# A decoder trunk on one core: the last steps of each layer norm taken through a PSUM bank, with nothing of them on GpSimd

## The chip, the cores and the metric

The kernel runs on one core of one Trainium2 chip. The metric is the device time of one execution in microseconds. A core has five engines, each with a queue of its own that it works through in order: TensorE (PE), which multiplies matrices and writes only to PSUM; VectorE (DVE); ScalarE (ACT); GpSimd (POOL); and SyncE (SP), which here only issues DMAs. Semaphores order the engines against each other. SBUF is the working memory; PSUM consists of eight banks per partition.

## The reference, cut to what matters

The reference is a stack of two decoder layers over 528 tokens (16 meta tokens and 512 tokens of the sequence), 1024 wide. Each layer has a half-step SwiGLU feed-forward block, a token mixer with three kinds of heads, and a second feed-forward block; behind each of the three stands a layer norm.

```python
def _layer_norm(x, g, b):
    xf = x.astype(F32)
    mu = jnp.mean(xf, axis=-1, keepdims=True)
    var = jnp.mean(jnp.square(xf - mu), axis=-1, keepdims=True)
    return ((xf - mu) * lax.rsqrt(var + LN_EPS) * g.astype(F32) + b.astype(F32)).astype(x.dtype)
...
    for l in range(DEPTH):
        h = _layer_norm(DEEPNORM_ALPHA * h + FFN_RES * _swiglu(h, ffn_w_gate[l, 0], ffn_w_up[l, 0], ffn_w_down[l, 0]),
                        ln_g[l, 0], ln_b[l, 0])
...
        mix = jnp.concatenate([o_lru, o_ssd, o_dn], axis=-1) @ w_out[l]
        h = _layer_norm(DEEPNORM_ALPHA * h + mix, ln_g[l, 1], ln_b[l, 1])
        h = _layer_norm(DEEPNORM_ALPHA * h + FFN_RES * _swiglu(h, ffn_w_gate[l, 1], ffn_w_up[l, 1], ffn_w_down[l, 1]),
                        ln_g[l, 2], ln_b[l, 2])
    return h[:, N_META:]
```

## The kernel before, in words

The tokens are cut into two halves, u = 0 (272 tokens) and u = 1 (256 tokens). Activations lie transposed: 128 channels on the partitions, eight tiles `m` for the 1024 channels, tokens along the row. A product in fp32 accuracy is made of three products of shortened numbers: each operand is split into a high part and a low part, `hh` and `hl` for the activations, and two halves of a `wt` tile for the weights. One product of a 128-column weight slab with the activations (`gemm`) is 24 matmuls into one tile `g` of PSUM: first the eight with the high weights and `hh`, then eight with the low weights and `hh`, and last eight with the high weights and `hl`. A slab comes by DMA into `wr`; ACT makes its high part, and POOL (four pieces) or DVE (one piece) the low part.

PSUM is dealt out in two pools: three banks with the tag `g` for these products, and five banks with the tag `c` for everything else: sums of the norms, and the small products of the mixer (the SSD blocks `ssd_block`, with tiles `s`, `s_sm`, `s_st`; the DeltaNet chain with `d_` and `db` tiles; the LRU).

A layer norm (`layer_norm`) of a half works on its eight tiles `acc[u][:, m]`: a matmul with ones gives the sum on all partitions (`mu`, a `c` bank); the tiles are centred, squared and summed (`ls`, `lq`); a chain of some fifteen tiny DVE steps on the tile `lv` makes the inverse root; matmuls of `lv` with the identity spread it over the partitions (`rp`, a `c` bank; in the trace `c<-ident,lv`). Then, for each of eight tiles: DVE scales it in place (`acc<-acc,par,c`), ACT adds the bias into `hh` (`hh<-acc,par`), DVE forms the low part `hl` as tile plus bias minus `hh` (`hl<-acc,par,hh`), and ACT adds the bias into the tile itself for the next residual (`acc<-acc,par`). For the tile m = 5 (`LN_POOL`) the last two are the other way about: ACT writes the tile, and POOL subtracts (`hl<-acc,hh`). There are ten such norms: three places in each of two layers, for two halves, less the last place, which another function does.

The order of the instructions on every engine is made at build time by a planner (`Recorder.schedule`). All instructions are recorded, each with a price from a table and a level, the length of what hangs on it; then the planner runs a clock for each engine and issues, where an engine is free, the ready instruction with the highest level. Tiles take a buffer of their pool when their first instruction is issued. A `c` tile that is not the oldest one still without a bank gets one only if more than three of the five are free (`SPARE`). Where the planner sees TensorE idle before a new `g` tile, it may put in matmuls of ones with ones (line 388), which compute nothing that is used. The two halves run a stage apart and are woven together, so that the products of one half fill TensorE while the mixer or the norm of the other goes through its chain.

Of the kernel before, what the change touches and what calls it, by code (L numbers as in the profile page):

```python
# [8 lines left out]
F32 = mybir.dt.float32  # L9
F32R = mybir.dt.float32r  # L10
I32 = mybir.dt.int32
AF = mybir.ActivationFunctionType
ALU = mybir.AluOpType
AX = mybir.AxisListType

P = 128
D = 1024
KD = 8
# [14 lines left out]
TILES = 6  # L33
DB_BUFS = 2
LRU_BUFS = 1
LN_POOL = (5,)
GROUPS = ((3, 3, 3, 3, 2), (3, 3, 3, 3, 2))
ALONE = ((2, 2, 2, 2), (2, 2, 2, 2))
POOL_SHARE = 0.7
# [360 lines left out]
class Trunk:  # L400
# [391 lines left out]
    def layer_norm(self, u, s, row, off=0, keep=False):  # L792

        nc = self.nc
        n = NTOK[u] - off
        a = [self.acc[u][:, m, off:] for m in range(KD)]
        mu = self.tl(self.psm, [P, 512], "c")[:, :n]
        nc.tensor.matmul(mu, self.ones, s, start=True, stop=True)
        s2 = [self.tl(self.wk, [P, 272], "ls2")[:, :n] for _ in range(2)]
        for m in range(KD):  # L800
            nc.vector.scalar_tensor_tensor(a[m], mu, -1.0 / D, a[m], ALU.mult, ALU.add)
            if m < 2:
                nc.scalar.activation(s2[m], a[m], AF.Square)
            else:
                q = self.tl(self.wk, [P, 272], "lq")[:, :n]
                nc.scalar.activation(q, a[m], AF.Square)
                if m % 2:
                    nc.gpsimd.tensor_tensor(s2[1], s2[1], q, ALU.add)
                else:
                    nc.vector.tensor_tensor(s2[0], s2[0], q, ALU.add)  # L810
        blocks = []
        c = 0
        while c < n:
            w = (n % P) if (c == 0 and n % P) else P
            blocks.append((c, w))
            c += w
        nb = len(blocks)
        vp = self.tl(self.psm, [P, 512], "c")
        v = self.tl(self.wk, [P, 3, 3], "lv")
        nc.vector.memset(v, 1.0)  # L820
        for i, (c, w) in enumerate(blocks):
            for q in range(2):
                nc.tensor.matmul(vp[:w, i:i + 1], s2[q][:, c:c + w], self.ones[:, 0:1], start=q == 0, stop=q == 1)
        if blocks[0][1] < P:
            w = blocks[0][1]
            nc.vector.tensor_scalar(v[:w, 0, 0:1], vp[:w, 0:1], 1.0 / D, LN_EPS, ALU.mult, ALU.add)
            nc.vector.tensor_scalar(v[:, 0, 1:nb], vp[:, 1:nb], 1.0 / D, LN_EPS, ALU.mult, ALU.add)
        else:
            nc.vector.tensor_scalar(v[:, 0, :nb], vp[:, :nb], 1.0 / D, LN_EPS, ALU.mult, ALU.add)
        self.rsqrt(v[:, 1, :], v[:, 0, :], v[:, 2, :])  # L830
        rp = self.tl(self.psm, [P, 512], "c")[:, :n]
        for i, (c, w) in enumerate(blocks):
            nc.tensor.matmul(rp[:, c:c + w], v[:w, 1, i:i + 1].to_broadcast([w, P]), self.ident[:w, :w], start=True, stop=True)
        g = [self.col(ROW_LN_G + row + m) for m in range(KD)]
        b = [self.col(ROW_LN_B + row + m) for m in range(KD)]
        hi = [self.hh[u][:, m, off:] for m in range(KD)]
        for m in range(KD):
            nc.vector.scalar_tensor_tensor(a[m], a[m], g[m], rp, ALU.mult, ALU.mult)
            nc.scalar.activation(hi[m], a[m], AF.Identity, bias=b[m])
        for m in range(KD):  # L840
            lo = self.hl[u][:, m, off:]
            if m in LN_POOL:
                nc.scalar.activation(a[m], a[m], AF.Identity, bias=b[m])
                nc.gpsimd.tensor_tensor(lo, a[m], hi[m].bitcast(F32), ALU.subtract)
            else:
                nc.vector.scalar_tensor_tensor(lo, a[m], b[m], hi[m].bitcast(F32), ALU.add, ALU.subtract)
                nc.scalar.activation(a[m], a[m], AF.Identity, bias=b[m])
        if keep:
            nc.sync.dma_start(self.res[u], self.acc[u])

# [790 lines left out]
```

## Time and profile before

| what | value |
|---|---|
| time, median of 3 runs | 2460.74 us (2446.69 to 2464.13) |
| the profiled execution: its time, its span | 2460.38 us, 2458.7 us |
| TensorE busy | 2312.6 us, 94% of the span |
| VectorE busy | 1504.2 us, 61% |
| ScalarE busy | 865.9 us, 35% |
| GpSimd busy | 883.0 us, 36% |
| mean granted clock of TensorE | 0.948 of full speed |

The span runs from the first to the last instruction; the time of the execution has 1.7 us more around it. The profile names an instruction by its line, its engine, and what it writes and reads (`hl<-acc,par,hh`). Since every instruction is issued by the planner, nearly all have line 390; the names of the tiles tell them apart. "Idle before" is the time that the engine stood still just ahead of an instruction, and the name behind the arrow is what it waited for. Matmuls overlap, so a row's duration is longer than what it adds: sixteen in 2.16 us begin 0.125 us apart.

### The profile page before, as it was taken

Reading aid. Unit: us, or ns where it says so; the run is one execution under the profiler, and the core shown is the slowest. Engines: PE = TensorE matmul, PEld = TensorE weight load, DVE = VectorE, ACT = ScalarE, POOL = GpSimd, SP = SyncE. Lnnn points to the kernel's source line nnn. Section 1 sums busy time; section 2 is a strip of 40 time slices with the busy share of each in tenths; the row PEclk is TensorE's granted clock in tenths of the full one; section 3 lists DMA queues with packets and bytes.
Section 4 is the critical chain, followed back from the end, with each engine's and each line's share of the span. In section 5 each row is a group of like instructions: output and inputs, shape, how many; then the busy total and the mean of one; then the engine's idle time right before and its main releaser. Section 6 shows DMA issues by size and latency. Waiting matters only on the chain.

```text
span 2458.7 us, 46832 instructions
## 1 busy us (share of the span) xinstructions
PE 2312.6 (94%) x18712; PEld 2199.1 (89%) x18712; DVE 1504.2 (61%) x3529; ACT 865.9 (35%) x1546; POOL 883.0 (36%) x1214
## 2 busy tenths in 40 slices
PE   8999998988899999999999999998989989999997
PEld 8999998876887999999999999988768878999996
DVE  6444467757867664444574444678577686654445
ACT  3222344442333454222242223443433444432222
POOL 5000566634545576000010005666445556640000
PEclk9999999987886999999999999999888989999999
DMA  6232454531341456233232334545314525552320
GB/s 169 78 103 87 131 145 144 146 97 35 110 108 54 139 157 186 86 104 95 68 95 80 91 91 138 156 139 141 97 35 118 142 61 155 172 168 90 91 90 35
DMA packets 426332, 271.99 MB, mean 111 GB/s; under 512 B 33421, under 2 KB 407921, under 8 KB 425857
## 3 DMA queue, kind: packets, MB, share of 16 engines
q1 hardware_dynamic: 425536, 268.83, 37.7%
q8 instruction: 147, 2.41, 0.4%
q0 software_dynamic: 576, 0.16, 0.1%
q14 instruction: 73, 0.59, 0.1%
HBM read 260.76 MB, written 8.19 MB: 109 GB/s over the span
## 4 chain that ended last, share of the span: by engine, by line
PE 70%; DVE 16%; DMA 4%; issue 3%; POOL 3%; ACT 3%; SPq 0%; POOLq 0%; DVEq 0%; ACTq 0%
PE g L390 61%; PE c L390 9%; POOL wt L390 2%; DVE wt L390 2%; DVE acc L390 2%; DVE fs L390 1%; DVE lru L390 1%; ACT wt L390 1%; DMA wr<-in_ffn_w_gate_dram 1%; DVE d_sq L390 1%; DVE s L390 1%; DMA wr<-in_ffn_w_up_dram 1%; DMA d_tx<-d_xd 1%; DVE sp L390 1%; DVE l_h L390 1%
## 5 line engine op out<-in xcount | busy, mean ns | idle before, releaser
L390 PE MATMUL g<-hh,wt 128*128 128x256 f32 (+1 forms) x7616 | 1063.7, 290 | 22.5 <-DVE fs L390 8.8
L390 PEld LDWEIGHTS g<-hh,wt 128*128 128x128 f32 x7616 | 985.4, 192 | 37.5 <-DVE fs L390 9.0
L390 POOL TENSOR_TENSOR wt<-wr,wt 128x256 fp32r<-128x256 f32 x884 | 681.8, 803 | 783.7 <-ACT wt L390 726.4
L390 ACT CAST wt<-wr 128x1024 fp32r<-128x1024 f32 x484 | 498.0, 1040 | 619.0 <-PE g L390 482.0
L390 PE MATMUL g<-hl,wt 128*128 128x256 f32 (+1 forms) x3808 | 562.7, 288 | 1.8 <-DVE hl L390 1.2
L390 PE MATMUL g<-hid,wt 128*128 128x256 f32 (+1 forms) x4224 | 543.7, 286 | 18.6 <-DVE hid L390 10.2
L390 PEld LDWEIGHTS g<-hid,wt 128*128 128x128 f32 x4224 | 524.4, 189 | 27.2 <-DVE hid L390 13.0
L390 PEld LDWEIGHTS g<-hl,wt 128*128 128x128 f32 x3808 | 505.3, 192 | 6.3 <-DVE hl L390 2.5
L390 DVE SCALAR_TENSOR_TENSOR acc<-g,acc 128x256 f32<-128x256 f32 (+1 forms) x608 | 256.7, 427 | 226.1 <-PE g L390 222.0
L390 DVE TENSOR_TENSOR wt<-wr,wt 128x1024 fp32r<-128x1024 f32 x263 | 335.0, 1285 | 88.1 <-ACT wt L390 86.8
L390 DVE SCALAR_TENSOR_TENSOR fs<-ft,g 128x272 f32<-128x272 f32 (+1 forms) x200 | 84.6, 423 | 188.8 <-ACT ft L390 188.0
L390 DVE TENSOR_TENSOR g<-fs,g 128x256 f32<-128x256 f32 (+1 forms) x176 | 76.4, 434 | 173.9 <-PE g L390 173.5
L390 ACT ACTIVATE ft<-g 128x272 f32<-128x272 f32 (+1 forms) x208 | 80.6, 388 | 281.6 <-PE g L390 249.2
L390 ACT CAST hid<-g 128x256 fp32r<-128x256 f32 (+1 forms) x176 | 65.8, 374 | 223.5 <-DVE g L390 223.2
L390 POOL TENSOR_TENSOR ls<-ls,lq 128x256 f32<-128x256 f32 (+1 forms) x30 | 27.6, 920 | 264.2 <-ACT lq L390 261.3
L390 DVE TENSOR_TENSOR hid<-g,hid 128x256 fp32r<-128x256 f32 (+1 forms) x176 | 74.9, 425 | 42.4 <-ACT hid L390 42.1
L390 POOL TENSOR_TENSOR wr<-wr,db 128x512 f32<-128x512 f32 x4 | 5.0, 1274 | 262.0 <-ACT wr L390 262.0
L390 DVE SCALAR_TENSOR_TENSOR fs<-g,par,fs 128x271 f32<-128x271 f32 (+1 forms) x144 | 69.1, 482 | 21.9 <-ACT halo L390 17.0
L390 ACT ACTIVATE fs<-g,par 128x272 f32<-128x272 f32 (+1 forms) x48 | 25.2, 524 | 67.4 <-PE g L390 57.9
L390 DVE SCALAR_TENSOR_TENSOR acc<-acc,par,c 128x256 f32<-128x256 f32 (+1 forms) x104 | 43.6, 480 | 8.6 <-PE c L390 8.5
L390 ACT ACTIVATE ft<-fs 128x272 f32<-128x272 f32 (+1 forms) x56 | 23.7, 423 | 58.6 <-DVE fs L390 58.6
L390 POOL TENSOR_TENSOR s<-s,s_sm 128x512 f32<-128x512 f32 (+1 forms) x20 | 22.0, 1105 | 61.6 <-ACT s L390 45.1
(305 smaller groups left out, 1742.4 us busy)
## 6 DMA issues: line engine op xcount, KB each, us to landing
wr<-in_ffn_w_gate_dram SPq DMA_DIRECT2D x120, 512.0 KB
wr<-in_ffn_w_up_dram SPq DMA_DIRECT2D x120, 512.0 KB
wr<-in_ffn_w_down_dram SPq DMA_DIRECT2D x120, 512.0 KB
wr<-in_w_in_dram SPq DMA_DIRECT2D x88, 512.0 KB
wr<-in_w_out_dram SPq DMA_DIRECT2D x32, 512.0 KB
res<-acc SPq DMA_DIRECT2D x2, 1088.0 KB
acc<-res SPq DMA_DIRECT2D x8, 272.0 KB
acc<-in_x_dram SPq DMA_DIRECT2D x4, 512.0 KB
```

Of the source, the lines that this page charges most:

```text
L390: op.fn(*[on(x) for x in op.args], **{k: on(x) for k, x in op.kw.items()})
```

## The change

The scaled tile is no longer written back in place, but into a `c` bank of PSUM of its own, one for each of the eight tiles. From that bank ACT takes `hh`, DVE takes `hl`, and ACT takes the sum that goes into the tile `acc`. All eight low parts are on DVE; the case for POOL is gone. The lines are written tile by tile, and the planner makes its order anew from the recorded instructions.

```diff
-LN_POOL = (5,)
...
         for m in range(KD):
-            nc.vector.scalar_tensor_tensor(a[m], a[m], g[m], rp, ALU.mult, ALU.mult)
-            nc.scalar.activation(hi[m], a[m], AF.Identity, bias=b[m])
-        for m in range(KD):
-            lo = self.hl[u][:, m, off:]
-            if m in LN_POOL:
-                nc.scalar.activation(a[m], a[m], AF.Identity, bias=b[m])
-                nc.gpsimd.tensor_tensor(lo, a[m], hi[m].bitcast(F32), ALU.subtract)
-            else:
-                nc.vector.scalar_tensor_tensor(lo, a[m], b[m], hi[m].bitcast(F32), ALU.add, ALU.subtract)
-                nc.scalar.activation(a[m], a[m], AF.Identity, bias=b[m])
+            t = self.tl(self.psm, [P, 512], "c")[:, :n]
+            nc.vector.scalar_tensor_tensor(t, a[m], g[m], rp, ALU.mult, ALU.mult)
+            nc.scalar.activation(hi[m], t, AF.Identity, bias=b[m])
+            nc.vector.scalar_tensor_tensor(self.hl[u][:, m, off:], t, b[m], hi[m].bitcast(F32), ALU.add, ALU.subtract)
+            nc.scalar.activation(a[m], t, AF.Identity, bias=b[m])
```

In the order, names carry numbers of their buffers: `acc_24_119` is the tile of half 0 and `acc_32_127` that of half 1; `c_121` to `c_125` are the five banks; one row of the matmuls stands for a run of alike ones (x8).

The first place is VectorE at the first norm of half 1 in layer 0 (538 us in the trace before). Before, from its scaling steps on:

```order
L390 SCALAR_TENSOR_TENSOR acc_32_127<-acc_32_127,par_103,c_123 128x256 x8
L390 TENSOR_TENSOR s_799_894<-c_121,t_y_630 16x512
L390 TENSOR_TENSOR s_800_895<-c_121,st_dtd_642 16x512
L390 TENSOR_TENSOR s_sm_899<-c_122,tri_105 16x16
L390 TENSOR_TENSOR s_sm_899<-c_123,tri_105 16x16
L390 SCALAR_TENSOR_TENSOR hl_5_100<-acc_32_127,par_103,hh_3_98 128x256 x7
L390 TENSOR_SCALAR s_806_901<-c_121,st_cs_641 16x16 x4
```

In the changed kernel, the end of the same norm (five scalings and four low parts stand ahead of these rows):

```order
L389 SCALAR_TENSOR_TENSOR c_121<-acc_32_127,par_103,c_123 128x256
L389 SCALAR_TENSOR_TENSOR hl_5_100<-c_125,par_103,hh_3_98 128x256
L389 SCALAR_TENSOR_TENSOR c_125<-acc_32_127,par_103,c_123 128x256
L389 SCALAR_TENSOR_TENSOR hl_5_100<-c_121,par_103,hh_3_98 128x256
L389 SCALAR_TENSOR_TENSOR c_121<-acc_32_127,par_103,c_123 128x256
L389 SCALAR_TENSOR_TENSOR hl_5_100<-c_125,par_103,hh_3_98 128x256
L389 TENSOR_TENSOR s_815_910<-c_123,t_y_638 16x512
L389 TENSOR_TENSOR s_816_911<-c_123,st_dtd_650 16x512
L389 TENSOR_TENSOR s_sm_915<-c_125,tri_105 16x16
L389 SCALAR_TENSOR_TENSOR hl_5_100<-c_121,par_103,hh_3_98 128x256
L389 TENSOR_TENSOR s_sm_915<-c_125,tri_105 16x16
L389 TENSOR_SCALAR s_822_917<-c_125,st_cs_649 16x16 x4
```

The first steps of half 0's SSD block (`s<-c,t_y` and the next ones) stood between the scalings and the low parts; now they stand behind all scalings and seven low parts, and the norm goes round on two banks, `c_121` and `c_125`, with `rp` in `c_123`. At the same norm of layer 1 (1763 us) the order changes in the same way, with all eight low parts ahead.

The second place is TensorE at the same norm. Before, from the last matmul of ones with `ls` to the first products of the SSD block:

```order
L390 MATMUL c_122<-ones_104,ls_480_575 128x1
L390 MATMUL g_145<-hh_2_97,wt_144 128x272 x7
L390 MATMUL g_145<-hl_4_99,wt_144 128x272 x8
L388 MATMUL c_123<-ones_104 128x128 x2
L390 MATMUL c_123<-ident_96,lv_876 128x128 x2
L390 MATMUL c_121<-ident_96,acc_24_119 16x128 x4
L390 MATMUL c_122<-ident_96,acc_24_119 16x128
L390 MATMUL c_122<-acc_24_119 16x16
L390 MATMUL c_123<-acc_24_119 16x16
L390 MATMUL c_121<-tri_105,st_adt_635 128x16 x2
```

In the changed kernel:

```order
L389 MATMUL c_121<-ones_104,ls_480_575 128x1
L389 MATMUL g_136<-hl_4_99,wt_135 128x272 x4
L389 MATMUL g_139<-hh_2_97,wt_158 128x272 x7
L389 MATMUL c_123<-ident_96,lv_884 128x128 x2
L389 MATMUL g_139<-hh_2_97,wt_158 128x272 x9
L389 MATMUL g_139<-hl_4_99,wt_158 128x272 x8
L389 MATMUL g_145<-hh_2_97,wt_133 128x272 x16
L389 MATMUL g_145<-hl_4_99,wt_133 128x272 x2
L389 MATMUL c_123<-ident_96,acc_24_119 16x128 x4
L389 MATMUL c_125<-ident_96,acc_24_119 16x128
L389 MATMUL c_125<-acc_24_119 16x16
L389 MATMUL g_145<-hl_4_99,wt_133 128x272 x6
```

The norm has moved ahead of products of half 0: 35 of their matmuls now stand between the spreading of `lv` and the SSD block's first products, where there was none, and six more behind those. Over the whole program the matmuls of ones on a `c` bank (line 388 before) go from 46 to 31, and those on a `g` bank from 13 to 12; every other matmul is there as often as before.

## Rows read from the trace of the kernel before

**Rows 1.** The page's head and part 1: busy time, share, instructions.

```profile
span 2458.7 us, 46832 instructions
PE 2312.6 (94%) x18712; PEld 2199.1 (89%) x18712; DVE 1504.2 (61%) x3529; ACT 865.9 (35%) x1546; POOL 883.0 (36%) x1214
```

**Rows 2.** The page's part 4: shares of the chain that ended last.

```profile
PE 70%; DVE 16%; DMA 4%; issue 3%; POOL 3%; ACT 3%; SPq 0%; POOLq 0%; DVEq 0%; ACTq 0%
```

**Rows 3.** The view of the cores: span and mean granted clock.

```profile
core 0: 2458.7 us, clock 0.948
```

**Rows 4.** Windows view: stretch, its length, each engine's busy time, PEclk.

```profile
538.90:576.50 37.60, 32.21 (x124) 21.20 (x125) 21.96 (x63) 12.52 (x30) 5.71 (x8) 0.50 0.14 43
```

**Rows 5.** Tile view of hl: min/median/max ns; then what its readers waited for.

```profile
L390 DVE SCALAR_TENSOR_TENSOR hl<-acc,par,hh x70: 464/492/1018, 365.6 to 2105.0; 128x256 fp32r<-128x256 f32 x42, 128x272 fp32r<-128x272 f32 x28
...
L390 POOL TENSOR_TENSOR hl<-acc,hh x10: 733/1068/3488, 365.8 to 2102.2; 128x256 fp32r<-128x256 f32 x6, 128x272 fp32r<-128x272 f32 x4
...
  DVE hl L390: 3.7, 8
...
  POOL hl L390: 1.4, 2
```

**Rows 6.** Groups of VectorE, all forms together: count, busy us, mean ns.

```profile
L390 DVE SCALAR_TENSOR_TENSOR acc<-acc,par,c 128x256 f32<-128x256 f32 (+1 forms) x104 | 43.6, 480 | 8.6 <-PE c L390 8.5
...
L390 DVE SCALAR_TENSOR_TENSOR hl<-acc,par,hh 128x256 fp32r<-128x256 f32 (+1 forms) x70 | 37.8, 597 | 0.0
```

**Rows 7.** Groups of ScalarE by form: count, busy us, mean ns.

```profile
L390 ACT ACTIVATE acc<-acc,par 128x256 f32<-128x256 f32 x48 | 21.2, 498 | 1.1 <-DVE hl L390 1.1
L390 ACT ACTIVATE hh<-acc,par 128x256 fp32r<-128x256 f32 x48 | 20.3, 496 | 2.9 <-DVE acc L390 2.9
...
L390 ACT ACTIVATE lru<-c,par 128x256 f32<-128x256 f32 x4 | 1.9, 474 | 3.9 <-DVE l_h L390 2.2 <-PE c L390 1.6
```

**Rows 8.** Timeline of TensorE at half 0's first norm: start, length, [idle before].

```profile
368.99 0.30 PE L390 MATMUL g<-hl,wt 128*16 128x272 f32 x1 [0.18 <-DVE hl L390]
369.88 0.42 PE L390 MATMUL g<-hl,wt 128*16 128x272 f32 x2 [0.59 <-DVE hl L390]
370.77 0.30 PE L390 MATMUL g<-hl,wt 128*16 128x272 f32 x1 [0.47 <-DVE hl L390]
```

**Rows 9.** Timeline of VectorE at half 1's first norm.

```profile
538.21 3.22 DVE L390 SCALAR_TENSOR_TENSOR acc<-acc,par,c 128x256 f32<-128x256 f32 x8
541.34 0.67 DVE L390 TENSOR_TENSOR s<-c,t_y 16x512 f32<-16x512 f32 x1
...
542.70 3.22 DVE L390 SCALAR_TENSOR_TENSOR hl<-acc,par,hh 128x256 fp32r<-128x256 f32 x7
545.85 1.21 DVE L390 TENSOR_SCALAR s<-c,st_cs 16x16 f32<-16x16 f32 x8
```

**Rows 10.** Timeline of TensorE at half 1's first norm.

```profile
527.30 2.16 PE L390 MATMUL g<-hh,wt 128*128 128x272 f32 x16
...
537.17 0.71 PE L390 MATMUL c<-ident,lv 128*128 128x128 f32 x4 [2.25 <-DVE lv L390]
...
541.48 0.23 PE L390 MATMUL c<-acc 64*16 64x16 f32 x2 [2.91 <-DVE acc L390]
542.67 3.59 PE L390 MATMUL c<-tri,st_adt 16*128 16x16 f32 x16 [0.95 <-DVE s L390]
```

**Rows 11.** The chain that ended last, in order of time: two of its pieces.

```profile
1263.81 2.29 POOL hl L390
...
1767.59 3.49 POOL hl L390
```

**Rows 12.** Timeline of GpSimd at half 1's first norm of layer 1.

```profile
1771.04 2.76 POOL L390 TENSOR_TENSOR wt<-wr,wt 128x256 fp32r<-128x256 f32 x4
1773.77 0.58 POOL L390 TENSOR_TENSOR s<-s,s_sm 16x64 f32<-16x64 f32 x2
```

**Rows 13.** Groups of instructions: the matmuls of ones.

```profile
L388 PE MATMUL c<-ones 128*128 128x128 f32 x92 | 17.2, 334 | 0.0
```

## The prediction

> **What bounds the kernel now.** I read the head of the page first. TensorE is busy for 94% of the span, the next engine, VectorE, for 61% [rows 1], and the chain that ended last runs through TensorE for 70% and through VectorE for 16% [rows 2]. The reader should take two things from this: over most of the span only fewer TensorE products would help, and the change takes none away; what it can move is the rest, the stretches in which TensorE waits for a chain on the other engines.
>
> The second thing to read is the clock. Its mean is 0.948 [rows 3], and it has two levels, 2.4 GHz (1.00) and 1.2 GHz (0.50). So some (1 - 0.948) / 0.5 x 2458.7 = 256 us of the span run at 1.2 GHz. The first of the long such stretches is 538.9 to 576.5 us: TensorE is busy for 32.2 of 37.6 us, at 0.50 [rows 4], and it begins right at the first norm of half 1, after TensorE had stood still for 2.25 us [rows 10]. At 2.4 GHz its busy time would be 16.1 us less. That is the price of one such stretch, and it is more than anything the norms' own instructions can give.
>
> The third view is the norms themselves. Readers of `hl` on TensorE waited 3.7 us for VectorE (eight times) and 1.4 us for GpSimd (twice), all told [rows 5]. Half 0's first norm shows how: `hl` tiles come some 0.9 us apart and three products wait 0.18, 0.59 and 0.47 us for them [rows 8]. At half 1's first norm the wait is not for `hl`; TensorE stands still for 2.25, 2.91 and 0.95 us because the SSD block's chain is queued on VectorE with the norm [rows 10].
>
> **The change part by part, by its own instructions.** VectorE: 70 low parts of 597 ns mean [rows 6] are 41.8 us. They take between 464 and 1018 ns, with a median of 492 [rows 5], so the mean is lifted by a part of them that takes twice as long; these lie where GpSimd works. A step of the same kind that has one operand in PSUM is the scaling, at 480 ns mean over both sizes [rows 6]. I take 480 for the new `hl`: 80 x 0.48 = 38.4 us, so VectorE does 3.4 us less in ten norms although it has ten instructions more. Bounds for the new `hl`: 464 ns, the least of the old (37.1 us in all), and 597 ns, should the slow ones stay (47.8 us): from 4.7 us less to 6.0 us more, spread over ten norms. I am near the first since the scaling runs in the same places. The scaling itself keeps its operands and only writes to a bank instead of SBUF; I cost that at nothing, bounded by 16 ns (480 less 464) either way on 80 instructions, 1.3 us.
>
> [...]
>
> ScalarE: 160 instructions read PSUM instead of SBUF. `hh` and `acc` take 496 and 498 ns at 256 columns [rows 7]; the like instruction from a bank, `lru<-c,par`, takes 474 [rows 7]. That is 22 ns x 160 = 3.5 us less on an engine that is not on the path (ACT has 3% of the chain [rows 2]); I count it as zero, and what covers it is TensorE's products.
>
> GpSimd: ten `hl` of 733 to 3488 ns go [rows 5]. Two of them stand on the chain that ended last, 2.29 and 3.49 us long [rows 11]. What is late next is known for the second: behind it in GpSimd's queue came four pieces of a weight, 2.76 us, and only then the SSD block's `s` [rows 12], for which TensorE stood. Without it the queue is 3.4 us earlier, but `s` also needs VectorE, which is later there (below). So I count no more than 1 us of each.
>
> Sum of this part: at half 0's first norm the 1.24 us of waits [rows 8] go, since 16 steps of 0.48 us are done in 7.7 us; the other waits for `hl` (3.9 us of 5.1 [rows 5]) go by about half, 2 us; GpSimd's two give 1 us each, of which I keep one. Together 4 us.
>
> **The order of the planner.** At half 1's first norm, before, VectorE ran eight scalings, then the SSD block's first steps 3.1 us after the norm's start (538.21 to 541.34), then seven `hl` [rows 9]. In the changed order those steps stand behind eight scalings and seven `hl`. A pair of tiles now needs four VectorE steps and four ScalarE steps on two banks. Eight scalings took 3.22 us, 0.40 each [rows 9]; so 15 steps take 6.0 us at least, and if the two banks make each pair wait through scaling, `hh` and `acc` one after the other (0.48 + 0.50 + 0.50 us [rows 6, 7], 1.5 us, under the 1.6 us of four VectorE steps) no more than some 7. The SSD block thus starts at 6.0 to 7.0 us in place of 3.1, some 3.5 us later; its next step, `s<-c,st_cs`, which stood behind all `hl` already (7.6 us after the start [rows 9]), some 1.5 us later.
>
> Against this, the norm now runs beside products. Before, nothing stood between the spreading of `lv` and the SSD block, and TensorE waited 2.91 and 0.95 us there [rows 10]. Now 35 matmuls stand between and six more behind. Sixteen matmuls begin 0.125 us apart [rows 10], so they are 5.1 us of work, more than the 3.5 us. As all of half 0's products are done by the start of the SSD block in either order, work that moves into the wait comes off the time: I take the 3.86 us of the two waits as gone, less 1.5 us for the later step: 2.4 us. Layer 1's norm of half 1 is moved in the same way; I take 1 us there, since one more low part and a weight's split stand ahead. The 2.25 us wait for `lv` stays; the change does not touch that chain.
>
> The fifteen matmuls of ones that go from `c` banks say the same from the planner's side: it puts them only where it sees TensorE idle. In the trace the 46 made 92 rows of 17.2 us [rows 13], so it sees about 15/46 x 17.2 = 5.6 us less idle time. I add nothing for it.
>
> **Sum.** 4 + 2.4 + 1 = 7.4 us, off the profiled execution's 2460.4 us: 2453 us. That execution lies at the median of the three runs shown (2460.7), so the sum is made on a typical one.
>
> **The rivals.** *One starved stretch more at 1.2 GHz (slower).* The mechanism is the banks and VectorE's order: the SSD chain waits for the norm, at half 1's norms of both layers. It decides where the moved products do not last as long as the delay: if their weights come late, the 5.1 us of cover shrink below 3.5. Then TensorE stands still for 3.5 us at both, the three norms that go round on two banks are some 1.5 us longer, and one more stretch like the one of 37.6 us is run at 1.2 GHz: 2460.4 + 7 + 4.5 + 16.1 = 2488 us. For it: the clock did fall just there before, and there are fewer matmuls of ones to keep TensorE at work. Against: the products moved there do the same service.
>
> *A stretch given back (faster by more).* Products inside the norm keep TensorE busy where the 37.6 us stretch began, and it stays at 2.4 GHz: 16.1 us on top of 7.4, 2437 us; with a further one shortened by half, 2429 us. For it: 35 matmuls stand where 2.25 + 2.91 + 0.95 us of idle time stood. Against: the SSD chain behind the norm has few products left to run beside it, in either order.
>
> *Nothing.* The norms' steps are hidden under products, half 0's norms above all, and the moved products are only missing elsewhere, in the DeltaNet chain just ahead: 2460 us. Should the new `hl` cost more than the old (the upper bound, 6.0 us), it comes out here as well. [...]
>
> **How the numbers follow.** A measurement of this kernel can tell about 1% from no change, 24.6 us. I give the forecast 0.50, nothing 0.21, a stretch given back 0.16, a stretch more 0.13. The forecast and nothing are within 1%; from the given-back stretch I count 2429 to 2437 as faster; the stretch more is slower. So faster 0.16, same 0.71, slower 0.13. The range takes in the forecast with its bounds (2453 plus 9.4 for dear low parts, less 1.3 for cheap ones), nothing, and most of both stretches; it ends at 2430 and 2484, half-way into the faster rival and a little short of the slower one, leaving out about 0.1 on each side.
>
> **What would show it right or wrong.** In the changed profile: `hl<-c,par,hh` at 470 to 490 ns, with no long ones, also where GpSimd works; no `hl` on GpSimd; waits of TensorE for `hl` near 2 us in all; between the spreading of `lv` and the SSD block of half 0 no idle time of TensorE over 1 us; about 31 matmuls of ones on `c` banks. The forecast is wrong if the mean granted clock moves by more than 0.01 (0.01 is 25 us at 1.2 GHz, about 12 us of time), or if the idle time lost at the norms turns up at the DeltaNet chain.

## The result, and the profile of the changed kernel

The changed kernel takes 2474.0 us, median of 16 runs (2459.0 to 2482.6), against 2458.5 us of the kernel before, also of 16 runs (2442.7 to 2464.1). The ratio is 1.0066, 95% interval 1.0045 to 1.0087: slower by 15.5 us. I had forecast 2453 us, 7 us faster. The time lies in the range; the sign was wrong.

The page of the changed kernel, its head, part 1 and the chain of part 4, answers to [rows 1, 2]:

```profile
span 2467.3 us, 46804 instructions
...
PE 2312.1 (94%) x18680; PEld 2203.5 (89%) x18680; DVE 1508.0 (61%) x3539; ACT 862.8 (35%) x1546; POOL 863.9 (35%) x1204
...
PE 69%; DVE 18%; issue 4%; POOL 3%; DMA 3%; ACT 3%; SPq 0%; POOLq 0%; DVEq 0%; ACTq 0%
```

TensorE's busy time is the same to 0.5 us, and GpSimd has 19 us less. VectorE has 3.8 us more, where 3.4 us less was forecast: its low parts did fall, from 41.8 us [rows 6] to 38.8 us (80 of 0.484 us, below), but other steps of it rose. The view of the cores [rows 3]:

```profile
core 0: 2467.3 us, clock 0.948
```

This one execution (2469.1 us with what lies around its span) has the clock of before and is 8.7 us longer. It is a good one of its kernel, 5 us under the median. Over all runs the clock did move. Each run lists its span and mean granted clock, so its time at 1.2 GHz is (1 - clock) / 0.5 x span, as in the prediction. The median of that is 277 us for the changed kernel and, in the five jobs of the experiments, 246 to 251 us for the one before. Half of the difference, 13 to 15 us, would be nearly the whole loss, but half is too much: among the runs of one and the same kernel, a microsecond more at 1.2 GHz goes with 0.34 us more of time (all kernels of this document pooled, each about its own mean; 0.31 for the changed kernel's 16 runs). By that rate 9 to 11 of the 15.5 us go with the clock, and the rest is elsewhere. Both sums are used again below. The clock records of both profiles hold 1.00 and 0.50 and nothing else. In the kernel before it is 0.50 from 723.3 to 760.8 us, where eight matmuls of 256 columns begin 0.214 us apart (756.89 to 758.60), and 1.00 from 100 to 384 us, where sixteen begin 0.119 us apart (100.32 to 102.23). The 1.2 GHz is an estimate from the first, 256 columns in 0.214 us, if a cycle does one column; 2.4 GHz is its double.

The norm's own instructions came out as forecast. The tile view of `hl` [rows 5], with what ended the waits of its readers:

```profile
L389 DVE SCALAR_TENSOR_TENSOR hl<-c,par,hh x80: 464/483/502, 360.8 to 2110.4; 128x256 fp32r<-128x256 f32 x48, 128x272 fp32r<-128x272 f32 x32
...
  DVE hl L389: 1.7, 4
```

The longest of eighty takes 502 ns, where some took 1018 ns before; the waits for `hl` in this view fell from 5.1 to 1.7 us. The view counts the waits of the weight loads along with those of the matmuls. The matmuls' own are smaller, in the view of TensorE's waits of the kernel before (first two lines) and of the changed one:

```profile
PE g L390 <- DVE hl L390: 1.2, 3, 0.6
PE g L390 <- POOL hl L390: 0.6, 1, 0.6
...
PE g L389 <- DVE hl L389: 0.7, 2, 0.5
```

So there were 1.8 us to gain here, and 1.1 us were gained. The groups by form [rows 6, 7, 13] have their mean in ns after the busy time:

```profile
L389 DVE SCALAR_TENSOR_TENSOR hl<-c,par,hh 128x256 fp32r<-128x256 f32 x48 | 21.7, 478 | 5.7 <-ACT acc L389 4.0 <-ACT hh L389 1.7
...
L389 ACT ACTIVATE hh<-c,par 128x256 fp32r<-128x256 f32 x48 | 21.4, 482 | 8.3 <-DVE c L389 8.1
...
L387 PE MATMUL c<-ones 128*128 128x128 f32 x62 | 12.4, 358 | 0.0
```

The timeline of TensorE at the first norm of half 0 (the first two lines) and of half 1 (the others) answers to [rows 8, 10]; idle time ahead of a line is in brackets:

```profile
366.23 0.98 PE L389 MATMUL g<-hid,wt 128*128 128x256 f32 x6 [0.94 <-DVE acc L389]
...
368.29 1.15 PE L389 MATMUL g<-hl,wt 128*16 128x272 f32 x8
...
520.86 1.05 PE L389 MATMUL c<-ones,ls 128*128 128x1 f32 x8 [2.71 <-DVE lv L389]
...
525.03 1.22 PE L389 MATMUL c<-ident,lv 128*128 128x128 f32 x4 [0.66 <-DVE lv L389]
...
533.60 0.71 PE L389 MATMUL c<-ident,acc 128*16 128x128 f32 x5 [1.72 <-DVE c L389]
...
536.23 1.95 PE L389 MATMUL c<-tri,st_adt 16*128 16x16 f32 x16
```

Half 0's eight products follow each other without the three waits of 1.24 us, but just ahead of them is a new one of 0.94 us. At half 1's norm 2.25 + 2.91 + 0.95 us of idle time became 0.66 + 1.72, and 2.71 us are new, ahead of the norm's sums: 6.11 us became 5.09. The timeline of VectorE there [rows 9] shows the price:

```profile
526.29 0.88 DVE L389 SCALAR_TENSOR_TENSOR c<-acc,par,c 128x256 f32<-128x256 f32 x2 [1.31 <-PE c L389]
...
533.45 0.48 DVE L389 SCALAR_TENSOR_TENSOR hl<-c,par,hh 128x256 fp32r<-128x256 f32 x1
534.24 0.68 DVE L389 TENSOR_TENSOR s<-c,t_y 16x512 f32<-16x512 f32 x1 [0.31 <-PE c L389]
...
537.77 1.21 DVE L389 TENSOR_SCALAR s<-c,st_cs 16x16 f32<-16x16 f32 x8 [1.28 <-PE c L389]
```

The SSD block starts 7.95 us after the norm (534.24 less 526.29), 3.1 before; its step `s<-c,st_cs` at 11.5 us, 7.6 before.

The same norm of layer 1, in TensorE's timeline of the kernel before:

```profile
1766.42 0.21 PE L390 MATMUL c<-acc 64*16 64x16 f32 x2 [0.92 <-DVE acc L390]
1767.61 3.50 PE L390 MATMUL c<-tri,st_adt 16*128 16x16 f32 x16 [0.98 <-DVE s L390]
...
1774.13 0.82 PE L390 MATMUL c<-s,s 16*64 16x16 f32 x10 [1.88 <-POOL s L390]
```

in that of the changed kernel, and three lines of VectorE's there:

```profile
1756.42 0.71 PE L389 MATMUL c<-ident,lv 128*128 128x128 f32 x4 [1.27 <-DVE lv L389]
...
1766.29 0.60 PE L389 MATMUL c<-ident,acc 128*16 128x128 f32 x4 [3.53 <-DVE c L389]
1767.29 0.28 PE L389 MATMUL c<-ident,acc 128*16 128x128 f32 x1 [0.40 <-DVE hl L389]
...
1768.02 0.23 PE L389 MATMUL c<-acc 64*16 64x16 f32 x2 [0.31 <-DVE hl L389]
1769.21 3.59 PE L389 MATMUL c<-tri,st_adt 16*128 16x16 f32 x16 [0.95 <-DVE s L389]
```

```profile
1757.17 0.88 DVE L389 SCALAR_TENSOR_TENSOR c<-acc,par,c 128x256 f32<-128x256 f32 x2 [0.80 <-PE c L389]
...
1761.60 0.88 DVE L389 SCALAR_TENSOR_TENSOR hl<-c,par,hh 128x256 fp32r<-128x256 f32 x2 [0.85 <-ACT hh L389]
...
1767.89 0.67 DVE L389 TENSOR_TENSOR s<-c,t_y 16x512 f32<-16x512 f32 x1
```

Here TensorE's idle time went up, from 3.78 us (0.92 + 0.98 + 1.88) to 6.46 us (1.27 + 3.53 + 0.40 + 0.31 + 0.95). The longest piece, 3.53 us, is an SSD product that waits for a bank which a scaling holds. Half 0's products had run out by then, and the SSD block started 10.7 us after the norm's first scaling.

**Where the time went.** The start of the norm that ends layer 0 and of the kernel's last norm, in VectorE's timeline of the kernel before:

```profile
1241.84 1.31 DVE L390 SCALAR_TENSOR_TENSOR acc<-acc,par,c 128x272 f32<-128x272 f32 x3
...
2095.07 2.43 DVE L390 SCALAR_TENSOR_TENSOR acc<-acc,par,c 128x256 f32<-128x256 f32 x6
```

and in that of the changed kernel:

```profile
1227.12 1.72 DVE L389 SCALAR_TENSOR_TENSOR c<-acc,par,c 128x272 f32<-128x272 f32 x4
...
2102.62 1.66 DVE L389 SCALAR_TENSOR_TENSOR c<-acc,par,c 128x256 f32<-128x256 f32 x4
```

Up to the end of layer 0 the changed kernel is 14.7 us ahead; at the last norm it is 7.5 us behind. In this pair of executions layer 1 lost 22 us. The windows view (length, busy time of PE, PEld, DVE, ACT, POOL, then PEclk) from 520 to 660 us and over layer 1, of before:

```profile
520.00:660.00 140.00, 118.71 (x766) 97.58 (x766) 103.80 (x293) 51.58 (x116) 60.68 (x87) 0.79 0.28 80
1217.00:2100.00 883.00, 825.80 (x6726) 775.87 (x6725) 587.18 (x1485) 337.10 (x633) 367.52 (x502) 0.94 0.39 110
```

and of the changed kernel:

```profile
520.00:660.00 140.00, 121.58 (x776) 102.93 (x777) 106.16 (x306) 51.09 (x111) 60.27 (x88) 0.78 0.25 73
1217.00:2100.00 883.00, 816.78 (x6514) 764.70 (x6514) 573.91 (x1442) 323.13 (x609) 346.79 (x488) 0.92 0.37 108
```

Around half 1's first norm the clock is where it was (0.79, 0.78), though TensorE's idle time at the norm fell by a microsecond; in layer 1 the clock fell from 0.94 to 0.92 (the fixed window doesn't hold quite the same work: 6726 and 6514 matmuls).

### The profile page after: what moved, and what is told of

Read it like the earlier page. It is cut to its first block, busy times and chain, and to the rows that moved or that the text cites. A ratio compares the mean times of both kernels' runs of the same rounds, so it can differ in the third digit from the quotient of the medians.

```text
span 2467.3 us, 46804 instructions
## 1 busy us (share of the span) xinstructions
PE 2312.1 (94%) x18680; PEld 2203.5 (89%) x18680; DVE 1508.0 (61%) x3539; ACT 862.8 (35%) x1546; POOL 863.9 (35%) x1204
## 4 chain that ended last, share of the span: by engine, by line
PE 69%; DVE 18%; issue 4%; POOL 3%; DMA 3%; ACT 3%; SPq 0%; POOLq 0%; DVEq 0%; ACTq 0%
PE g L389 59%; PE c L389 9%; POOL wt L389 3%; DVE wt L389 2%; DVE fs L389 2%; DVE acc L389 1%; ACT wt L389 1%; DVE lru L389 1%; DVE d_ss L389 1%; DVE hl L389 1%; DVE s L389 1%; DVE sp L389 1%; DVE d_sq L389 1%; DMA wr<-in_ffn_w_up_dram 1%; DVE db L389 1%
## 5 line engine op out<-in xcount | busy, mean ns | idle before, releaser
L389 ACT ACTIVATE hh<-c,par 128x256 fp32r<-128x256 f32 (+1 forms) x80 | 36.2, 491 | 18.9 <-DVE c L389 18.7
```

Of the source, the lines that this page charges most:

```text
L389: op.fn(*[on(x) for x in op.args], **{k: on(x) for k, x in op.kw.items()})
```

## The experiments

All were run beside the kernel before, whose median was 2457.6 to 2462.1 us in the five jobs, so medians compare across them. The change does three things: it gives the scaled tile a place of its own, that place is a PSUM bank, and GpSimd does no `hl`. With them comes a new order from the planner. The recorded expectations name their theories by letters; the ones that lasted are B (the banks are the price), V (a separate scaled tile with few buffers) and S (single plans scatter, and the design has no part in it). V has this meaning only in the last two expectations; before that it stands for everything in the change but the banks. Many of the recorded ranges were missed: the second, third, fourth, fifth, seventh, sixteenth and eighteenth kernel came out in none that theirs state.

**One layer at a time.** The bank route for some norms, the old route in place for the rest:

```
e1:  if row < 24:   # bank route, else the old one
e2:  if row >= 24:
```

> The PSUM route in layer 0 only (four norms), the old steps in layer 1; the planner makes its order anew. Theory O (the loss is the planner's new order in layer 1's mixer, between 1600 and 2100 us; layer 0's order is a gain of some 11 us): about 2447 us, 11 less than before. Theory B (the scaled tiles hold banks that the mixer needs, in both layers alike): about half of the loss, 2466 us. Theory N (the route itself costs, norm for norm): four of ten norms, 2465 us.

> The old steps in layer 0, the PSUM route in layer 1 and at the layer's border only (six norms). Theory O: the loss without layer 0's gain, 2476 to 2484 us. Theory B: about half of the loss, 2466 us. Theory N: six of ten norms, 2468 us.

The condition covers six norms in the first (layer 0's, with those that end it) and four in the second, not the numbers given there. The first took 2450.3 us, ratio 0.9967 (0.9943 to 0.9991); the second 2455.3 us, 0.9979 (0.9957 to 1.0002). The first one's plan of layer 0 is the changed kernel's, the second one's is that of before. Layer 0's gain is real: the norm that ends layer 0 starts at 1222 to 1234 us in the profiles of the six kernels with the changed kernel's plan there (the changed kernel and the first, third, fifth, sixth and twelfth), and at 1241 to 1243 us in the three with that of before. But the second has the bank route just where the changed kernel loses 22 us, and isn't slower; its plan of layer 1 is again another. That the new route in layer 1 is by itself the loss falls.

**Without single norms.** The condition leaves out the last two norms, or half 1's norm in layer 1's mixer, at 1757 us:

```
e5:  if row != 32:
e6:  if (row, u) != (24, 1):
```

> The PSUM route in all norms but the last two, those behind layer 1's mixer; layer 0 is planned as in the changed kernel, and layer 1 nearly so (2.6% of TensorE's rows differ). Theory P (the loss sits in the plan of layer 1 that follows when its first two norms take the PSUM route, and is paid as a longer time at 1.2 GHz): 2470 to 2476 us. Theory B (banks held by the last two norms are what hurts): 2455 to 2462 us.

> The PSUM route in all norms but half 1's first norm of layer 1 (the one at 1763 us); layer 1's plan differs from the changed kernel's in 13% of TensorE's rows. Theory P in its local form (the SSD block's steps pushed behind this norm's low parts are the loss): 2450 to 2458 us, as with the PSUM route in layer 0 only. Theory S (each new plan is a draw, between 2445 and 2475 us, and no one place is at fault): anywhere between, most likely not at either end.

They took 2466.3 us, 1.0043 (1.0020 to 1.0065), and 2462.7 us, 1.0027 (1.0007 to 1.0047). Each takes back 8 to 11 us of the 15.5. As each also has a new plan behind the norm that it leaves out, this doesn't say what one norm costs.

**The same order, one part changed.** The planner's order is kept as it came out, and only the operands change. In the third kernel the scaled tile lies in SBUF, in buffers that the other half may still hold, so its values are not the reference's; the order and the instructions are the changed kernel's. In the fourth, order and buffers are those of before, and GpSimd's ten `hl` are issued on VectorE:

```
e3:  real = self.tags["wk.lq" if m % 4 < 2 else "wk.ls2"].real[m % 2]
e4:  fn = self.nc.vector.tensor_tensor if op.seq in self.moved else op.fn
```

> The changed kernel's order kept instruction for instruction (the planner still deals out the PSUM banks), but the scaled tile is put into four SBUF buffers (lq and ls2) in place of the bank. Theory O: the order is the same, so the loss stays; the low parts meet GpSimd again: 2474 to 2482 us. Theory N: without PSUM the loss goes, 2460 us.

> The order of the kernel before kept instruction for instruction, but GpSimd's ten low parts are issued on VectorE in their place. Theory O: hardly any difference, 2455 to 2461 us. Theory N in the form that VectorE's ten further low parts are what costs: 2464 us or more.

They took 2466.1 us, 1.0029 (1.0003 to 1.0056), and 2451.2 us, 0.9975 (0.9952 to 0.9997). So at one order the banks cost some 8 us, and taking GpSimd out gains some 6 to 8. Both are small beside what follows, and neither makes 15 us of loss.

**Other tables for the planner.** `MARGIN` is what the planner adds to its lags. A new table moves the order and leaves every instruction as it is:

```
-MARGIN = (20, 5, 5, 5, 0)
+MARGIN = (20, 10, 10, 10, 0)   # e7 (before), e8 (changed)
+MARGIN = (30, 5, 5, 5, 0)      # e10 (before), e9 (changed)
```

> The kernel before with another table MARGIN of the planner (20, 10, 10, 10, 0 in place of 20, 5, 5, 5, 0: hand-overs between engines priced 5 ns dearer): no instruction is changed, only the order. Theory S: the time moves by 5 to 15 us, to either side. Theory P: within 4 us of before, 2455 to 2463 us.

> The changed kernel with the same other table MARGIN (20, 10, 10, 10, 0): the change is whole, only the order differs. Theory S: the loss was this plan's, so the time falls back to 2450 to 2465 us. Theory N or B (the change itself costs, through its instructions or its banks): 2470 us or more again.

> The changed kernel with a third table MARGIN (30, 5, 5, 5, 0). Theory S alone (each plan is a draw, the change has no price of its own): as likely under 2459 us as over it. Theory S with a price of the change (two whole-change plans stand at 2474 and 2490 us so far): 2465 us or more.

> The kernel before with the third table MARGIN (30, 5, 5, 5, 0). Theory S alone: a draw, between 2435 and 2480 us. Theory S with a price of the change: under 2465 us, and under the changed kernel with the same table.

Before took 2436.5 us (0.9921, 0.9894 to 0.9947) and 2437.6 us (0.9911, 0.9888 to 0.9933); the changed kernel 2490.0 us (1.0127, 1.0096 to 1.0158) and 2465.2 us (1.0027, 1.0005 to 1.0048). A new order alone is worth 22 us to the kernel before. The change costs 15, 53 and 28 us under the three tables: its sign is firm, its size in any one plan is not. The view of the cores of the seventh and of the eighth kernel:

```profile
core 0: 2434.6 us, clock 0.961
```

```profile
core 0: 2495.7 us, clock 0.940
```

(1 - 0.961) / 0.5 x 2434.6 is 190 us at 1.2 GHz, (1 - 0.940) / 0.5 x 2495.7 is 299 us. But the second is the slowest of its kernel's six runs; the medians over the runs are 190 and 274 us. By the rate of 0.34, the 84 us between them go with 29 of the 53 us.

**The second table's order, no banks.** As the third kernel (and its values likewise not the reference's), at the order of the eighth:

> The order of the changed kernel with the second table MARGIN (the one at 2490 us), kept instruction for instruction, with the scaled tile in four SBUF buffers in place of its bank. These buffers may still be held by the other half's norm, so values are overwritten and the output is not the reference's; the work is the same. Theory B (in the run, the mixer's chain waits for banks that the norm's readers give back late): 8 us less or more, 2482 us or under, as with the first plan (2474 to 2466). If banks are no matter: within 4 us of 2490.

It took 2482.4 us, 1.0091 (1.0068 to 1.0115), 7.6 us under the eighth, as the third is 7.9 under the changed kernel. Each time the two intervals overlap a little; together they make the banks' 8 us likely. The view of TensorE's waits shows a wait that only the banks bring, its SSD product for a bank that a scaling holds; in the eighth kernel:

```profile
PE c L389 <- DVE c L389: 12.8, 2, 6.5
```

Its two waits are 6.46 and 6.36 us, at half 1's first norm of each layer. Without the banks this line is gone, but all the waits of that view, those for DMAs left out, still sum to 141.5 us, 141.1 with the banks: what this wait leaves, others take.

**More matmuls of ones.** My guess, which no run shows, was that TensorE's idle time, where the planner sees it, brings the clock down; then more of these matmuls should keep it up. The changed kernel, its own order, 93 of them in all in place of 43 (31 of the 43 are the `c` ones above):

```
+extra = max(0, int((s - free[e]) / (128 * 4 / 2.4) + 0.5))
+order += [new[0]] * extra if new else []
```

> The changed kernel's plan, with 93 matmuls of ones in place of 43 in the idle time that the planner sees. Theory C (the loss is time at 1.2 GHz, and matmuls in the idle time take it away): less time at the lower clock than 277 us, and half of what that falls by off the time: 2458 to 2468 us. If they stand where other work is then late: 2474 us or more.

2478.3 us, 1.0072 (1.0046 to 1.0099), and 272 us at 1.2 GHz for 277. More of them didn't bring the clock back, so the fewer matmuls of ones are an unlikely cause. That the added ones made other work late, the expectation's second case, isn't ruled out.

**A separate tile, but in SBUF.** The planner knows of it and makes its order for it; two buffers, which the norm's squares also use; the three tables:

```
-            t = self.tl(self.psm, [P, 512], "c")[:, :n]
+            t = self.tl(self.wk, [P, 272], "lq")[:, :n]
```

> The changed kernel with the scaled tile in two SBUF buffers (lq) that the planner knows of, so that no norm takes a c bank for it; all else of the change stays (a tile of its own, order tile by tile, nothing on GpSimd), and the planner makes its order anew. Theory B (the price of the change is that the planner must share the mixer's five banks with the norms): near before, 2445 to 2462 us. Theory V (the price is the rest: all low parts on VectorE, steps tile by tile): 2465 us or more.

> The same with the second table MARGIN, where before has 2437 us and the changed kernel 2490. Theory B: 2435 to 2455 us. Theory V: 2470 us or more.

> The same with the third table MARGIN, where before has 2438 us and the changed kernel 2465. Theory B: 2435 to 2452 us. Theory V: 2460 us or more.

2459.0 us (1.0014, 0.9993 to 1.0036), 2474.1 us (1.0066, 1.0028 to 1.0105) and 2491.3 us (1.0145, 1.0110 to 1.0181). The mean is 2474.8 us; the changed kernel's over the same tables is 2476.4. That the place of the tile is the price (theory B) falls for the mean over plans, though under the first table the SBUF tile does come out level with before.

**No separate tile, no GpSimd.** The kernel before with VectorE doing every `hl`, in place, the three tables:

```
-LN_POOL = (5,)
+LN_POOL = ()
```

> The kernel before with the second table MARGIN and all low parts on VectorE (LN_POOL empty), in place and in two loops as before; the planner makes its order anew. Theory V in the form that the ten further low parts on VectorE are the price: 2455 us or more. Theory B, or V in the form of the order tile by tile: 2430 to 2450 us.

> The kernel before with no low part on GpSimd: scaled tile, both parts and the sum all in place in SBUF, VectorE does all eighty low parts, planned afresh under the table that before and after use. Written in one loop tile by tile, as in the change, this kernel comes out in the same order instruction for instruction, so the code's order is no part of it; what it lacks of the change is a separate scaled tile. Theory V (a separate scaled tile with few buffers makes the planner finish tile by tile, and that order is the price): near before and near the frozen order without GpSimd (2451), 2440 to 2462, and 12 or more under the separate tile in SBUF (2459) or PSUM (2474) in the mean over the three tables. Theory G (taking GpSimd's low parts out makes the plan worse, the tile has no part in it): 2465 to 2485. Theory S (every new plan is one draw of a wide scatter and the design has no part in it): anywhere from 2437 to 2490, and the three no-GpSimd in-place plans scatter about 2460 as the others do.

> The same kernel planned under the third table, (30, 5, 5, 5, 0), under which before took 2438, the change 2465 and the scaled tile in own SBUF buffers 2491. Theory V: 2435 to 2460, well under 2465 and 2491. Theory G: 2465 to 2490, no better than the change. Theory S: no relation to either; with the run of the first table and 2452 of the second, a mean over the three tables near 2460 or above, inside the other designs' scatter.

By the order of the runs this is the second table first: 2451.8 us (0.9985, 0.9960 to 1.0010), then 2434.8 us under the first (0.9896, 0.9832 to 0.9961) and 2463.0 us under the third (1.0039, 1.0006 to 1.0073). Written in one loop, tile by tile as the change has it, but in place, this kernel comes out in the same order, instruction for instruction on TensorE, VectorE and ScalarE. So the way that the loop is written is no part of the price. The last of the three runs is a miss for theory V, which gave it 2435 to 2460 us and well under the change's 2465. All four designs, medians in us:

| design | table 1 | table 2 | table 3 | mean | at 1.2 GHz, mean of the medians |
|---|---|---|---|---|---|
| before | 2458.5 | 2436.5 | 2437.6 | 2444.2 | 213 |
| in place, no GpSimd | 2434.8 | 2451.8 | 2463.0 | 2449.9 | 219 |
| own tile in SBUF | 2459.0 | 2474.1 | 2491.3 | 2474.8 | 247 |
| own tile in a bank (the change) | 2474.0 | 2490.0 | 2465.2 | 2476.4 | 265 |

Read by columns. An own tile in SBUF costs 24, 22 and 28 us more than in place, nearly the same each time; by the intervals one such difference is uncertain by 11 to 17 us, their mean of 25 by some 8. The change itself costs 39 and 38 us more than in place without GpSimd under the first two tables, but 2 us, within the noise, under the third. A bank in place of SBUF costs 15, 16 and then -26 us more: no sign that holds. GpSimd's removal costs -24, 15 and 25 us: none either. These intervals hold only the scatter of runs; the scatter of plans is larger, since a single plan lies up to 17 us from its design's mean (theory S has this part of the truth). What stands against it is the mean over plans: 2475.6 us for the six with a separate tile and 2447.0 us for the six without, with a standard deviation of 12 to 13 us in each six. The 29 us between them are some four times their standard error of 7. So the separate tile is what costs (theory V), in the mean and not in every plan. Nor is it a price for each norm: the first two kernels have it in six and in four norms and aren't slower than before.

**What the separate tile does** is seen in VectorE's timeline at half 0's first norm. In place, without GpSimd (table 1):

```profile
359.01 0.91 DVE L390 SCALAR_TENSOR_TENSOR acc<-acc,par,c 128x272 f32<-128x272 f32 x2 [1.24 <-PE c L390]
...
360.17 1.72 DVE L390 SCALAR_TENSOR_TENSOR acc<-acc,par,c 128x272 f32<-128x272 f32 x4
...
363.87 0.49 DVE L390 SCALAR_TENSOR_TENSOR acc<-acc,par,c 128x272 f32<-128x272 f32 x1
...
364.61 0.49 DVE L390 SCALAR_TENSOR_TENSOR hl<-acc,par,hh 128x272 fp32r<-128x272 f32 x1
...
365.35 4.64 DVE L390 SCALAR_TENSOR_TENSOR hl<-acc,par,hh 128x272 fp32r<-128x272 f32 x7
```

in the changed kernel:

```profile
358.87 0.91 DVE L389 SCALAR_TENSOR_TENSOR c<-acc,par,c 128x272 f32<-128x272 f32 x2 [1.24 <-PE c L389]
...
360.84 0.90 DVE L389 SCALAR_TENSOR_TENSOR hl<-c,par,hh 128x272 fp32r<-128x272 f32 x2
...
364.94 0.91 DVE L389 SCALAR_TENSOR_TENSOR c<-acc,par,c 128x272 f32<-128x272 f32 x2
```

with the own tile in SBUF (table 1):

```profile
359.24 0.91 DVE L389 SCALAR_TENSOR_TENSOR lq<-acc,par,c 128x272 f32<-128x272 f32 x2 [1.23 <-PE c L389]
...
360.39 0.91 DVE L389 SCALAR_TENSOR_TENSOR hl<-lq,par,hh 128x272 fp32r<-128x272 f32 x2
...
369.26 0.90 DVE L389 SCALAR_TENSOR_TENSOR lq<-acc,par,c 128x272 f32<-128x272 f32 x2
```

In place, all eight scalings come first and the low parts, which are wanted later, after them: 5.4 us from the first to the end of the last scaling. With a separate tile the third scaling needs a free buffer, so low parts and sums stand between: 7.0 us with banks, 10.9 us with two SBUF buffers. And `hh`, the part that the first products read, comes with the scaling. Over the ten norms, from the start of the first `hh` to the end of the eighth in ScalarE's records, the mean is 4.4 to 4.8 us in the six in-place plans, 7.3 to 7.6 in the three with banks, 13.4 to 15.0 in the three with own SBUF buffers. The view of TensorE's waits, for `hh`, in the same three kernels:

```profile
PE g L390 <- ACT hh L390: 4.7, 6, 1.6
```

```profile
PE g L389 <- ACT hh L389: 8.3, 10, 2.5
...
PE c L389 <- DVE c L389: 5.2, 2, 3.5
```

```profile
PE g L389 <- ACT hh L389: 14.8, 16, 5.5
```

Under the other two tables the waits for `hh` are 9.7 and 4.9 us in the changed kernel, 3.0 and 3.6 us in place without GpSimd, 7.9 and 4.8 us in the kernel before, and 16.4 and 20.5 us with own SBUF buffers. The wait for a bank that a scaling holds is 5.2 and 12.8 us in the changed kernel under the first two tables and is absent under the third, where the change costs next to nothing against in place. These waits are the part of the price that is seen directly, and they are less than all of it.

## Why the prediction was wrong

**Right.** The low parts (forecast 480 ns, measured 478 and 494 by size, none long); none on GpSimd and 31 matmuls of ones (62 rows), as the order already had them. Layer 0 by itself gained, and more than the whole forecast: 14.7 us in the profiled run, and the kernel with the new route in its six norms is faster.

**The sum, place by place.** At half 0's first norm the forecast 1.24 us went, but 0.94 us of new waiting stands ahead: 0.3 us. At half 1's first norm of layer 0 the sum has 2.4 us; idle time went from 6.11 to 5.09 us, so 1.0 us. The 2.25 us that were to stay shrank to 0.66, of the 3.86 us that were to go 1.72 stayed, and 2.71 us are new, so what was gained came by another way than the one forecast; the mark "no idle time of TensorE over 1 us" failed by the 1.72. At the same norm of layer 1 the sum has 1 us off; idle time grew by 2.7 us. The term for the other waits for `hl` rests on a misreading: 3.7 and 1.4 us [rows 5] count the waits of weight loads along with those of matmuls, and the matmuls' own were 1.8 us in all. "Together 4 us" was more than there was.

**Mis-sized.** The step `s<-c,st_cs` is 3.8 us later, where I took 1.5: VectorE's fifteen steps took 7.6 us (526.29 to 533.93) for the 6.0 to 7.0 that I allowed.

**The step that failed** is the one on ScalarE, "I count it as zero, and what covers it is TensorE's products", with the bound that I drew from it: a norm on two banks takes "no more than some 7" us, and at layer 1's norm "I take 1 us there". I priced ScalarE's instructions by length and not by when they give a bank back and when the last `hh` is there. At layer 1's norm the round took 10.7 us (1757.17 to 1767.89): VectorE waited six times for ScalarE to be done with a bank or an `hh`, 2.74 us in all, and split a weight between. TensorE's products didn't cover it; it stood still for 3.53 us, and the 1 us gain became 2.7 us more waiting. I charged the round to the SSD block alone, while it holds for every norm: eight `hh` in 7.6 us for 4.5 in the mean of ten. And the sum left the rest of the order and the time at 1.2 GHz as they were; the planner moved work in the whole of the mixers, layer 1 lost 22 us in the profiled pair, and over the runs the time at 1.2 GHz rose to 277 us, from 246 to 251.

**The rivals.** "One starved stretch more at 1.2 GHz" had the sign and part of the mechanism: at half 1's norm of layer 1 the moved products didn't last as long as the delay, and TensorE stood still for 3.53 us, 1.72 us in layer 0. That they ran out was not for late weights, its condition, but for the longer round; and its one more stretch of 16.1 us isn't seen as such, so its 2488 us is 14 too many. That the time lies in the range is owed to this rival's share of it. "A stretch given back" fell: the 37.6 us stretch [rows 4] went, but from 520 to 660 us the clock stayed at 0.78. My mark "the mean granted clock moves by more than 0.01" would have missed the cause: it is 0.948 in both profiles, and in the median of the runs 0.944 for 0.949 to 0.950. The other mark, idle time at the DeltaNet chain, didn't come true either: TensorE's waits for the tiles `db` and `d_...` fell from 30 to 23 us, and those for the SSD block's `s...` rose from 19 to 28.

**What stays open.** In the profiled pair, which has the same time at 1.2 GHz (256 us), TensorE's waits grew from 122 to 131 us, those for DMAs left out, and that is the 8.7 us between the two: `hh` and the banks' `c` gave 9 of it (13.5 for 4.1), the others even out. Over the runs the time at 1.2 GHz comes on top: it is 46 us more than in place for the change in the mean of the tables, 28 us for the tile in SBUF, which by the rate of 0.34 goes with 16 of 27 and 10 of 25 us. What brings down the clock in layer 1 I couldn't tell; and the loss isn't proportional to how late `hh` is, as the SBUF tile, twice as late, costs the same. That the late `hh` and the banks' round are what the separate tile costs is thus shown for the waits and only argued for the rest. A norm in after's order but in place, or an own tile with eight buffers, would tell; neither was tried.

## What to carry to other kernels

Where a planner or scheduler makes the order, a scratch tile with few buffers is a constraint on the order, not only an operand: ask when the last of what the next stage reads is there, not only how long each step takes. Judge such a change under several neutral settings of the planner, since one plan can lie 15 us or more from its mates; even three settle only what is well above that. The fastest kernels here are the one with `hl` kept off GpSimd, in place, under the first table (2434.8 us, 0.9896, 0.9832 to 0.9961) and before under the second (2436.5 us). And count the time at the lower clock over several runs before a difference of half a per cent is explained from one profile.

## What the runs showed of the hardware

One kernel in one order doesn't have one time at 1.2 GHz: the changed kernel's 16 runs have 231 to 303 us of it, and take 2459 to 2483 us. From plan to plan the median goes from 190 to 279 us, and the time rises with it. But a microsecond at 1.2 GHz isn't half a microsecond lost: among runs of one kernel the rate is 0.34. By it, the 40 us that the six plans with a separate tile have more at 1.2 GHz (256 for 216 in the mean) go with 14 of the 29 us that they take longer.

In these traces the norm's low parts on VectorE take over 700 ns only where both their inputs lie in SBUF. The tile view in the kernel without GpSimd's `hl`, in place, where GpSimd still splits weights:

```profile
L390 DVE SCALAR_TENSOR_TENSOR hl<-acc,par,hh x80: 464/492/2209, 364.6 to 2082.9; 128x256 fp32r<-128x256 f32 x48, 128x272 fp32r<-128x272 f32 x32
```

One of them takes 2209 ns. In the kernel before, all 16 of the seventy that take over 700 ns run beside GpSimd's work for two thirds of their time or more, and the longest that doesn't run beside it takes 496. With one operand in a bank the longest of eighty took 502, though 17 of them ran beside it for more than half of their time. At the changed kernel's own order with the tile in SBUF (the third kernel) the longest is 974 again. Yet the kernel with the 2209 ns is the fastest of all, so what the even `hl` are worth is small beside its plan. With one source in a bank a low part was no longer than an even one without: the least is 464 ns with a bank (the changed kernel) and without one (the kernel above), the median 483 and 492 ns.
